# A state-space scan stage whose tensor-engine order is written out by hand, with 32-column output tiles

## The chip, the cores and the metric

One core of a Trainium2 chip (trn2) runs the whole program. The metric is the device time of one execution in microseconds (us), from start to end, as the median of several runs. PE is the tensor engine, DVE the vector engine, ACT the scalar engine, POOL the GpSimd engine, SP the engine that issues most DMAs. A PE matmul takes a stationary operand (loaded beforehand, up to 128x128) and streams a moving one through it into a PSUM bank; other engines must read PSUM before a bank can be used again.

## The reference

One decoder layer for a prompt of 512 tokens and 8 sample sequences of 8 tokens (576 tokens together, D = 1024): half a SwiGLU feed-forward, one wide input projection, a Mamba-2 state-space branch and an attention branch in parallel, their gated merge, an output projection, and half a SwiGLU again. The change concerns the state-space branch, cut here to what matters:

```
z, xbc, dt_raw, q, k, v, f_raw, g_ssd, g_att = split_combined(xn @ p['w_in'])
xc, conv_new = causal_conv(xbc, conv_prev, p['conv_w'], p['conv_b'])       # 4 taps, then SiLU
xs, Bm, Cm = jnp.split(xc, [D_SSM, D_SSM + SSD_GROUPS * D_STATE], axis=-1)  # 2048 + 4*128 + 4*128 columns
...
cb = jnp.einsum('bclgn,bcsgn->bclsg', Cc, Bc)
y_diag = jnp.einsum('bclsgr,bcsgrp->bclgrp', cb[..., None] * decay, xdt)
states = jnp.einsum('bclgn,bclgr,bclgrp->bcgrpn', Bc, jnp.exp(acs[:, :, -1:] - acs), xdt)
...
y_off = jnp.einsum('bclgn,bcgrpn,bclgr->bclgrp', Cc, h_prev, jnp.exp(acs))
y = (y_diag + y_off) + d_skip * xh
...
yg = y * silu(z); yg = yg * rsqrt(mean(yg * yg) + eps)                      # norm over each group
merged = sigmoid(g_ssd) * (y_ssd @ w_ssd_proj) + sigmoid(g_att) * (y_att @ w_attn_proj)
```

There are 32 heads of 64 channels in 4 groups; a chunk is 128 tokens, so the prompt has 4 chunks and the 64 sample tokens make a fifth.

## The kernel before

Activations lie transposed, channels on partitions and the 576 tokens along the free axis. Every large projection is a sum of three fp32r matmuls for each block of 128 input channels (`mm3`, lines 204 to 210): both operands are split into a high and a low part (`split` on lines 167 to 175 for weights, ACT makes the high part `whi`, DVE or POOL in turn the low part `wlo`), and high x high, high x low and low x high are added up in PSUM. A projection tile of 128 output channels covers the tokens in two halves of 288, each in a PSUM bank of its own (`acc`, two buffers): 24 matmuls a half for an input of 1024 channels, 12 for one of 512. DVE takes each half out of PSUM under `soon()`, which raises an instruction's priority for the scheduler.

The stages in order: first feed-forward; time steps and decays; attention, in which PE follows an order written by hand (`manual_schedule`, line 980) with half-tile pieces of other projections between its steps; group 0's convolutions and the attention output projection; the state-space scan; merge and output projection; second feed-forward. Outside the attention stage a scheduler sets the order of every engine, by its own estimate of when operands are ready. Each engine then works through its instructions strictly in that order.

The scan stage (line 1340 on) runs four groups. For each:

- `group_in(g)` (1078) makes six tiles with `conv_tile` (1036): the projections of B, C and four of x. The projection goes to `xr`; a PE transpose of its last columns into the second half's own bank (1059), copied out by ACT (`tt`, 1061), gives the new convolution state; ACT, three DVE steps of `kf` (1072), a tanh on ACT and two DVE writes (1074, 1076) give the convolved tile.
- `group_scan(g)` (1139) handles the samples as chunk 4 first and then chunks 0 to 3. `chunk` (1196) makes C.B (1202) and masks it into `cbm` (DVE, 1204), loads the cumulated decays `ab` by DMA, makes `dk` from them (ACT 1214 and 1215, DVE 1216), turns x (1225) and B (1232) by PE transposes, scales x to `xdt` and `xde` (DVE), and then forms y in one PSUM bank: for each of 8 heads one matmul of 64 columns from the chunk itself (1241) and, from chunk 1 on, one from the carried state (1243). DVE adds the skip (1245), and `gate` (1150) multiplies by the gate and sums squares on POOL and ACT. `carry` (1251) makes the next state, `state` (1265) updates one pair of heads of the samples' own states: transposes of a loaded state `h` (1273), an output product (1277), an update product (1280), and a DMA back.
- `halves` splits y into `ygh` and `ygl`; the samples' part is added and gated at the end of the group.
- `group_out(g)` (1320) finds the row scale of the group's norm (`rowscale`, 253: two matmuls with ones on lines 257 and 259, then a chain of small DVE operations up to 265), and projects y: 8 tiles with two halves of 12 matmuls, taken out by DVE (1331, 1334) and added to `accs` (1336).

The outer loop says in which order the work is written:

```
for g in range(4):
    cur = nxt
    gated = group_scan(g, *cur)
    if g < 3:
        nxt = group_in(g + 1)
    for _ in range((3, 0, 0, 5)[g]):
        j = next(late)
        gate_tile(gs, j, 8 + j)
    group_out(g, *gated)
```

The eight tiles of the gate projection (`gate_tile`, 507) are spare work: three go with group 0 and five with group 3.

PSUM banks in this stage: two `acc`, two `mm` (C.B, transposes of x and B, carry), two `tr` (states, row scales) and two `pv` (y and sample outputs).

## Time and profile before

| | us |
|---|---|
| runs shown (3) | 1911.07, 1919.22, 1919.95 |
| median | 1919.22 |
| the profiled execution | 1914.71 |
| its span, first to last instruction | 1912.9 |
| mean granted PE clock | 0.988 |

The profile is of one execution. Busy time counts an instruction's whole duration; matmuls are pipelined, so a busy PE may still work below its peak, and the time from one matmul's start to the next is the better measure. An fp32 matmul leaves two records, an fp32r matmul or a transpose one. In a row of a group, "idle before" is the time that the engine stood still just ahead of these instructions, and behind it stands what ended it. In a timeline row the first number is the start, the second the duration, "xN" the number of records merged, and a bracket gives the wait before it. A granted clock of 1.00 is full speed.

### The profile page before, as it was taken

How to read it: one execution, taken by the hardware profiler on the slowest of the kernel's cores; microseconds unless marked ns; L12 is line 12 of the kernel's file. 1: busy time of each engine (PE TensorE's matmuls, PEld its weight loads, DVE VectorE, ACT ScalarE, POOL GpSimd, SP SyncE). 2: the span in 40 equal slices, each digit the busy share in tenths (PEclk: the TensorE clock that was granted, in tenths of full speed). 3: DMA queues.
4: the chain of work that ended last, by engine and by line, in shares of the span. 5: the costliest groups of instructions: out<-in, count | busy, mean ns of one | idle time of the engine just before them, and what ended most of it. 6: DMA issues, size and time to landing. Idle time of an engine off the chain costs nothing. (4 is left out here: it accounts for less than half of the span.)

```text
span 1912.9 us, 38609 instructions
## 1 busy us (share of the span) xinstructions
PE 1840.0 (96%) x15335; PEld 1731.7 (91%) x15335; DVE 1065.6 (56%) x2204; ACT 748.2 (39%) x1553; POOL 652.2 (34%) x719
## 2 busy tenths in 40 slices
PE   7999999999998999999998988989999999999999
PEld 7999999999896888888997877878889999999998
DVE  4554334445234777775729767888785544334432
ACT  4233223334222555554427455555434333223322
POOL 0433012322322344432227455675744233003310
PEclk9999999999998999999999999999999999999999
DMA  5432223234534787865465545464654332222322
GB/s 152 112 96 80 89 78 89 83 105 111 145 109 129 188 255 223 246 200 148 95 174 153 141 127 142 111 178 124 174 155 136 89 88 77 80 74 81 88 90 71
DMA packets 270841, 243.21 MB, mean 127 GB/s; under 512 B 53276, under 2 KB 243404, under 8 KB 270508
## 3 DMA queue, kind: packets, MB, share of 16 engines
q1 hardware_dynamic: 208208, 169.35, 32.4%
q10 hardware_dynamic: 53092, 36.79, 6.4%
q0 software_dynamic: 9360, 34.61, 5.6%
q8 instruction: 121, 1.98, 0.4%
q14 instruction: 60, 0.49, 0.1%
HBM read 204.97 MB, written 29.03 MB: 122 GB/s over the span
## 5 line engine op out<-in xcount | busy, mean ns | idle before, releaser
L173 ACT ACTIVATE whi<-stage 128x512 fp32r<-128x512 f32 (+2 forms) x474 | 294.6, 622 | 732.4 <-PE acc L209 640.6
L208 PE MATMUL acc<-xh,whi 128*128 128x288 f32 x1856 | 561.7, 303 | 17.8 <-DVE xr L1046 11.5
L209 PE MATMUL acc<-xl,whi 128*128 128x288 f32 x1856 | 552.6, 298 | 0.0
L210 PE MATMUL acc<-xh,wlo 128*128 128x288 f32 x1856 | 552.3, 298 | 0.0
L174 DVE TENSOR_TENSOR wlo<-stage,whi 128x512 fp32r<-128x512 f32 (+1 forms) x373 | 271.9, 729 | 263.9 <-ACT whi L173 243.8
L208 PEld LDWEIGHTS acc<-xh,whi 128*128 128x128 f32 x1856 | 351.0, 189 | 24.8 <-DVE xr L1046 11.5
L209 PEld LDWEIGHTS acc<-xl,whi 128*128 128x128 f32 x1856 | 351.3, 189 | 2.1 <-issue 1.5
L210 PEld LDWEIGHTS acc<-xh,wlo 128*128 128x128 f32 x1856 | 350.7, 189 | 2.0 <-issue 1.3
L338 POOL TENSOR_TENSOR u<-u,s 128x288 f32<-128x288 f32 x88 | 92.1, 1048 | 484.3 <-DVE u L337 427.7
L208 PE MATMUL pv<-xh,whi 128*128 128x288 f32 (+1 forms) x784 | 231.4, 296 | 2.4 <-ACT xh L220 2.2
L209 PE MATMUL pv<-xl,whi 128*128 128x288 f32 (+1 forms) x784 | 231.9, 296 | 0.6 <-DVE xl L218 0.6
L210 PE MATMUL pv<-xh,wlo 128*128 128x288 f32 (+1 forms) x784 | 231.6, 296 | 0.0
L174 POOL TENSOR_TENSOR wlo<-stage,whi 128x512 fp32r<-128x512 f32 (+1 forms) x101 | 138.2, 1368 | 269.6 <-ACT whi L173 255.6
L208 PEld LDWEIGHTS pv<-xh,whi 128*128 128x128 f32 (+1 forms) x784 | 147.3, 188 | 2.9 <-ACT xh L220 2.4
L209 PEld LDWEIGHTS pv<-xl,whi 128*128 128x128 f32 (+1 forms) x784 | 147.2, 188 | 1.2 <-DVE xl L218 0.8
L210 PEld LDWEIGHTS pv<-xh,wlo 128*128 128x128 f32 (+1 forms) x784 | 147.2, 188 | 0.2
L340 POOL TENSOR_TENSOR hl<-u,hh 128x288 fp32r<-128x288 f32 x88 | 77.5, 882 | 81.6 <-ACT hh L339 81.6
L208 PE MATMUL pv<-hh,whi 128*128 128x288 f32 x352 | 104.4, 296 | 0.0
L209 PE MATMUL pv<-hl,whi 128*128 128x288 f32 x352 | 104.3, 296 | 0.0
L208 PE MATMUL acc<-hh,whi 128*128 128x288 f32 x352 | 104.1, 296 | 0.0
L210 PE MATMUL acc<-hh,wlo 128*128 128x288 f32 x352 | 104.1, 296 | 0.0
L209 PE MATMUL acc<-hl,whi 128*128 128x288 f32 x352 | 104.1, 296 | 0.0
(335 smaller groups left out, 3470.0 us busy)
## 6 DMA issues: line engine op xcount, KB each, us to landing
stage<-in_w_in_dram SPq DMA_DIRECT2D x52, 512.0 KB
stage<-in_ffn_w_up_dram SPq DMA_DIRECT2D x44, 512.0 KB
stage<-in_ffn_w_gate_dram SPq DMA_DIRECT2D x43, 512.0 KB
stage<-in_ffn_w_down_dram SPq DMA_DIRECT2D x40, 512.0 KB
pb<-pastD SPq DMA_DIRECT2D x32, 256.0 KB
ab<-cumD SPq DMA_DIRECT2D x32, 256.0 KB
h<-in_state_ssm_dram SPq DMA_DIRECT2D x32, 256.0 KB
out_dram<-h ACTq DMA_DIRECT2D x32, 256.0 KB
```

The source lines that it names most:

```text
L173: act(hi, view, AF.Copy)
L174: e.tensor_tensor(lo, view, hi.bitcast(F32), ALU.subtract)
L208: mm(out, lhsT=hi, rhs=a, start=first and i == 0, stop=False)
L209: mm(out, lhsT=hi, rhs=b, start=False, stop=False)
L210: mm(out, lhsT=lo, rhs=a, start=False, stop=last and i == n - 1)
L338: G.tensor_tensor(u, u, sil[half], ALU.mult)
L340: G.tensor_tensor(hl[:, hs(half)], u, hh[:, hs(half)].bitcast(F32), ALU.subtract)
```

## The change

The arithmetic stays the same. What changes is the code's order and, in the scan stage, who sets PE's order:

- `conv_tile` becomes a generator that yields after every 12 matmuls, and what follows the projection (transpose, copy, convolution steps) is put into a function `rest` that is called after the first piece of the next tile.
- `stream` runs a list of projection tiles as one stream of pieces, with the next tile's weights split and those of the tile after that loaded ahead. All projections of the stage go through it: each group's six tiles (`GroupIn`), the output projections (`GroupOut`) and the gate tiles.
- `group_scan` becomes a class `Scan` whose steps are called one by one: `front` (C.B, transposes, decays), `y`, `carry`, `state_load`, `state_turn`, `state_add`, `state_out`, `samples`, `final`. `front` transposes x and B straight behind C.B, ahead of the decays.
- In `y` each head's 64 output columns are made by two matmuls of 32 columns, and the order is four of the chunk's own, then four of the carried state, on the four column positions 0, 32, 64, 96.
- The whole stage stands in `manual_schedule` for PE: what the code writes is PE's order. Between the steps stand 12 slots a group, each filled with an equal share of the group's pieces. Group g's output projection now runs beside the scan of group g + 1, and the gate tiles are spread: two in group 0, one each in groups 1 and 2, four in group 3. The last group's output projection follows after the scan.

```diff
+    def halves_of(a, w, half):
+        for k in (0, 4):
+            mm3(a, w[k:k + 4], xs[k:k + 4], half, first=k == 0, last=k == 4)
+            if k == 0:
+                yield
...
-    def conv_tile(ct, w, prev, out):
+    def conv_tile(ct, w, prev, out, later):
...
         a = acc()
-        mm3(a, w, xs, 0)
+        yield from halves_of(a, w, 0)
         with soon():
             V.tensor_tensor(xr[:, 3:3 + HT], a, rbc[:, hs(0)], ALU.mult)
+        yield
...
+        def rest():
...
+        later.append(rest)
+        yield
...
+    def stream(jobs):
+        later = []
+        jobs[0][0].load(jobs[0][1])
+        ahead = jobs[0][0].get(jobs[0][1])
+        if len(jobs) > 1:
+            jobs[1][0].load(jobs[1][1])
+        for n, (_, _, body) in enumerate(jobs):
+            w, due, later = ahead, later, []
+            for c, _ in enumerate(body(w, later)):
+                if c == 0:
+                    for f in due:
+                        f()
+                    if n + 1 < len(jobs):
+                        ahead = jobs[n + 1][0].get(jobs[n + 1][1])
+                    if n + 2 < len(jobs):
+                        jobs[n + 2][0].load(jobs[n + 2][1])
+                yield
+        for f in later:
+            f()
...
-                for r in range(8):
-                    ov = yb[(r % 2) * 64:(r % 2 + 1) * 64, (r // 2) * n:(r // 2 + 1) * n]
-                    mm(ov, lhsT=xdt[:n, r, :], rhs=dks[r // 4][:n, r % 4, :n], start=True, stop=not 0 < c < 4)
-                    if 0 < c < 4:
-                        mm(ov, lhsT=hst[:, r, :], rhs=abs_[r // 4][:, r % 4, :], start=False, stop=True)
+                for i in range(4):
+                    for own in ((True, False) if 0 < c < 4 else (True,)):
+                        for e in range(2):
+                            r = 2 * i + e
+                            for q in range(2):
+                                o = e * 64 + q * 32
+                                ov = yb[o:o + 32, i * n:(i + 1) * n]
+                                if own:
+                                    mm(ov, lhsT=xdt[:n, r, q * 32:(q + 1) * 32], rhs=dks[r // 4][:n, r % 4, :n], start=True, stop=not 0 < c < 4)
+                                else:
+                                    mm(ov, lhsT=hst[:, r, q * 32:(q + 1) * 32], rhs=abs_[r // 4][:, r % 4, :], start=False, stop=True)
...
+        work = [[ins[1].job(i) for i in range(6)] + [gate_job(0), gate_job(1)],
+                [ins[2].job(0), ins[2].job(1)] + [outs[0].job(j) for j in range(8)] + [ins[2].job(i) for i in range(2, 6)] + [gate_job(2)],
+                [ins[3].job(0), ins[3].job(1)] + [outs[1].job(j) for j in range(8)] + [ins[3].job(i) for i in range(2, 6)] + [gate_job(3)],
+                [gate_job(4), gate_job(5)] + [outs[2].job(j) for j in range(8)] + [gate_job(6), gate_job(7)]]
...
+        with tc.manual_schedule(engines={mybir.EngineType.PE}):
+            for g in range(4):
...
+                sc.front(4)
+                fill()
+                if g:
+                    outs[g - 1].scale()
+                sc.front(0)
+                sc.state_load(0, 0)
+                fill()
+                sc.y(4, None)
+                for c in range(5):
+                    before = sc.carry(c) if c < 4 else None
+                    if c:
+                        sc.state_turn(c - 1)
+                    else:
+                        sc.state_load(1, 0)
+                    fill()
+                    if c < 3:
+                        sc.front(c + 1)
+                    if c:
+                        sc.state_add(c - 1)
+                        if c < 4:
+                            sc.state_load(0, c)
+                            sc.state_load(1, c)
+                    fill()
+                    if c < 4:
+                        sc.y(c, before)
+                    if c:
+                        sc.state_out(c - 1)
+                    if c == 2:
+                        sc.halves(0)
+                sc.final()
+                sc.samples()
+        outs[3].scale()
+        for _ in filler:
+            pass
```

Three places show how PE's order moves. A row has the line, the operation, output<-inputs, and the output's shape; L208 to L210 are projections, and a number behind a name tells one buffer from another.

The first is `front`. Before, in group 0, C.B of a chunk (L1202) is followed by y of the chunk ahead (L1241), then come the transposes of x (L1225) and of B (L1232):

```order
L1254 MATMUL mm_12518<-xde_12492,bt_12496 128x512
L1202 MATMUL mm_12560<-cT_11363,bT_11279 128x128
L1241 MATMUL pv_12498<-dk_12469,xdt_12490 64x128 x4
L1059 MATMUL acc_13072<-ident_76,xr_13043 91x128
L1241 MATMUL pv_12498<-dk_12478,xdt_12490 64x128 x4
L1225 MATMUL mm_12586<-ident_76,xg_11447 128x128 x4
L1232 MATMUL mm_12595<-ident_76,bT_11279 128x128
L1273 MATMUL tr_12525<-ident_76,h_2291_12523 128x128 x4
```

In the changed kernel C.B (L1261), the transposes of x (L1267) and of B (L1274) stand next to each other, and the samples' update products (L1363) follow:

```order
L1069 MATMUL acc_12828<-ident_76,xr_12723 91x128
L1261 MATMUL mm_12894<-cT_11364,bT_11295 128x128
L1267 MATMUL mm_12898<-ident_76,xg_11444 128x128 x4
L1274 MATMUL mm_12907<-ident_76,bT_11295 128x128
L1363 MATMUL tr_12933<-bs_12419,xs_12417 128x512
L1363 MATMUL tr_12937<-bs_12431,xs_12429 128x512
```

All three of `front`'s outputs are `mm` banks, of which there are two: the transpose of B takes the one that C.B was written to.

The second is y of chunk 1 of group 0, with 64-column tiles whose own and carried parts alternate (L1241 and L1243):

```order
L1280 MATMUL tr_12555<-bs_12447,xs_12445 128x512
L1241 MATMUL pv_12599<-dk_12566,xdt_12591 64x128
L1243 MATMUL pv_12599<-ab_12564,hst_12520 64x128
L1241 MATMUL pv_12599<-dk_12566,xdt_12591 64x128
L1243 MATMUL pv_12599<-ab_12564,hst_12520 64x128
```

and in the changed kernel with 32-column tiles in fours (L1314 and L1316), with the samples' outputs (L1373), the carry (L1328) and the state transposes (L1352) behind them:

```order
L1314 MATMUL pv_12985<-dk_12702,xdt_12692 32x128 x4
L1316 MATMUL pv_12985<-ab_12700,hst_12639 32x128 x4
L1314 MATMUL pv_12985<-dk_12702,xdt_12692 32x128 x4
L1316 MATMUL pv_12985<-ab_12700,hst_12639 32x128 x4
L1314 MATMUL pv_12985<-dk_12713,xdt_12692 32x128 x4
L1316 MATMUL pv_12985<-ab_12711,hst_12639 32x128 x4
L1314 MATMUL pv_12985<-dk_12713,xdt_12692 32x128 x4
L1316 MATMUL pv_12985<-ab_12711,hst_12639 32x128 x4
L1373 MATMUL pv_13030<-hT_12817,cz_12359 32x128 x4
L1373 MATMUL pv_13030<-hT_12825,cz_12359 32x128 x4
L1328 MATMUL mm_13040<-xde_12905,bt_12909 128x512
L1352 MATMUL tr_13045<-ident_76,h_2370_12941 128x128 x4
```

Twice as many matmuls make y, and no projection stands among them any more.

The third is the end of the last group's scan. Before, the transposes of the samples' output (L1302) and the first matmul of the row scale (L257) stand inside gate tiles (`xh`, `xl`):

```order
L1302 MATMUL tr_17209<-ident_76,oo_16761 128x128
L210 MATMUL acc_17448<-xh_4423,wlo_17440 128x288
...
L257 MATMUL tr_17565<-ssq_16683,cst_75 128x512
L210 MATMUL acc_17448<-xh_4770,wlo_17444 128x288
...
L259 MATMUL mm_17567<-ssq_16683,cst_75 128x64
L208 MATMUL acc_17511<-xh_4596,whi_17502 128x288
```

In the changed kernel no gate tile is left there, and the last output projection (`ygh`, `ygl`) follows at once:

```order
L1373 MATMUL pv_17782<-hT_17684,cz_12359 32x128 x4
L1398 MATMUL tr_17792<-ident_76,hst_17493 128x128 x4
L1385 MATMUL tr_17804<-ident_76,oo_17240 128x128 x3
L208 MATMUL acc_17854<-ygh_17475,whi_17729 128x288
...
L1385 MATMUL tr_17804<-ident_76,oo_17240 128x128
L257 MATMUL tr_17830<-ssq_16632,cst_75 128x512
L208 MATMUL acc_17876<-ygh_17475,whi_17729 128x288
L259 MATMUL mm_17832<-ssq_16632,cst_75 128x64
L209 MATMUL acc_17876<-ygl_17476,whi_17729 128x288
```

One half of a tile (acc_17854) stands between the samples' output and the row scale.

344 lines of the change are left out of this document (199 added, 145 removed).

## The prediction

> **What bounds the kernel now.** I read the page first, then a table of stages, then the groups of TensorE (PE) by line, and last the timeline at single places.
>
> ```profile
> PE 1840.0 (96%) x15335; PEld 1731.7 (91%) x15335; DVE 1065.6 (56%) x2204; ACT 748.2 (39%) x1553; POOL 652.2 (34%) x719
> ```
>
> PE is busy 96% of the span, so only what PE waits for, runs at a low clock, or spends on badly packed matmuls can be won. The stage table (columns: busy us and instructions of PE, weight loads, DVE, ACT, POOL; then granted clock, DMA share, GB/s) says where that is. 620:875 is the attention stage, whose PE order is written by hand already; 900:1000 holds group 0's convolutions; 1000:1432 is the scan with its projections, whose PE order the scheduler makes.
>
> ```profile
> 620.00:875.00 255.00, 249.28 (x3257) 213.72 (x3251) 192.69 (x563) 137.04 (x339) 100.17 (x129) 1.00 0.76 218
> 900.00:1000.00 100.00, 94.62 (x691) 92.57 (x690) 54.36 (x90) 33.38 (x54) 28.41 (x41) 0.98 0.46 119
> 1000.00:1432.00 432.00, 393.58 (x3140) 349.96 (x3139) 345.78 (x640) 227.85 (x525) 260.46 (x260) 0.98 0.52 146
> 1062.00:1080.00 18.00, 14.38 (x96) 12.43 (x94) 11.46 (x22) 9.79 (x24) 8.44 (x14) 0.81 0.59 143
> 1120.00:1136.00 16.00, 10.97 (x92) 9.57 (x90) 11.77 (x10) 4.19 (x10) 6.97 (x7) 0.89 0.45 121
> 1262.00:1280.00 18.00, 13.93 (x112) 11.31 (x112) 14.98 (x23) 13.39 (x36) 10.05 (x12) 0.91 0.57 144
> ```
>
> The scan stage leaves PE idle for 432 - 393.6 = 38.4 us, 9%; the hand-ordered attention stage for 255 - 249.3 = 5.7 us, 2.2%, at a similar DVE load (76% against 80%). What ends the waits in the scan stage, by group (idle is the last column):
>
> ```profile
> L208 PE MATMUL acc<-xh,whi 128*128 128x288 f32 x403 | 123.8, 307 | 13.2 <-DVE xr L1046 10.3 <-ACT tt L1061 2.3 <-ACT wdec L1135 0.5
> L208 PE MATMUL acc<-ygh,whi 128*128 128x288 f32 x253 | 78.1, 309 | 4.6 <-DVE u L1334 4.5
> L1241 PE MATMUL pv<-dk,xdt 128*64 128x128 f32 (+1 forms) x320 | 33.1, 280 | 8.8 <-DVE dk L1216 7.5 <-DVE xdt L1228 1.2
> ```
>
> Four single waits make 14.8 us of it:
>
> ```profile
> 1068.86 0.61 PE L208 MATMUL acc<-xh,whi 128*128 128x288 f32 x1 [3.55 <-DVE xr L1046]
> ...
> 1129.46 0.49 PE L1241 MATMUL pv<-dk,xdt 128*64 128x128 f32 x2 [5.03 <-DVE dk L1216]
> ...
> 1188.30 0.40 PE L208 MATMUL acc<-xh,whi 128*128 128x288 f32 x1 [3.09 <-DVE xr L1046]
> ...
> 1270.90 0.40 PE L208 MATMUL acc<-xh,whi 128*128 128x288 f32 x1 [3.17 <-DVE xr L1046]
> ```
>
> Three of the four have a low granted clock beside them (the last three rows of the table): 18 x 0.19 + 16 x 0.11 + 18 x 0.09 = 6.8 us of full clock.
>
> **The change, part by part.** Numbers of instructions stay the same on DVE, ACT, POOL and SP; PE alone gets more, smaller matmuls. The sum is made against the profiled execution, 1914.7 us (span 1912.9).
>
> *Waits that go.* With projection pieces between every step and its use, the four waits above and most small ones should go: all 38.4 us are up for removal. What is late next:
>
> (a) In `front`, the transpose of B (L1274) takes the PSUM bank that `cbm` is still read from, and only L1261 and four transposes stand between; nothing can pass it, and the whole stream behind it waits. DVE has to read `cbm`, often after an eviction of a projection:
>
> ```profile
> L1204 DVE TENSOR_TENSOR cbm<-mm,cst x20: 174/282/293, 995.1 to 1362.3; 128x128 f32<-128x128 f32 x16, 64x64 f32<-64x64 f32 x4
> ...
> L1334 DVE TENSOR_TENSOR u<-acc,ssq 128x288 f32<-128x288 f32 x46 | 20.8, 451 | 14.7 <-PE acc L210 8.1 <-POOL accs L1336 5.2 <-PE mm L1225 1.0
> ...
> L1072 DVE SCALAR_TENSOR_TENSOR kf<-xr,P,kf x72: 796/842/2022, 909.9 to 1316.4; 128x600 f32<-128x600 f32 x72
> ```
>
> How long the four transposes give it (from the first to the transpose of B, 0.49 us):
>
> ```profile
> 1017.44 0.66 PE L1225 MATMUL mm<-ident,xg 128*128 128x128 f32 x4
> 1017.93 0.27 PE L1232 MATMUL mm<-ident,bT 128*128 128x128 f32 x1
> ```
>
> 0.45 + 0.28 = 0.73 of DVE against 0.49 leaves 0.24 us; I take 0.45, for the hand-overs between engines and what else DVE has in hand, 20 times: 9 us. Bounds: 0, if DVE is free, and 20 x 1.1 = 22 if a convolution step (0.842) stands ahead as well.
>
> (b) The last convolution tile of a group is now followed by one gate tile alone in groups 1 and 2, and the next group's first transposes read it. I let its three steps (3 x 0.842) come out uncovered, twice: 5 us, bounds 0 and 16 (DVE having all of the group's start to do at once).
>
> (c) The end. Five gate tiles now run while the last samples are gated and the last row scale is found; the changed kernel has spent them earlier.
>
> ```profile
> 1387.43 0.27 PE L1302 MATMUL tr<-ident,oo 128*128 128x128 f32 x1
> ...
> 1391.80 0.32 POOL L1159 TENSOR_TENSOR ssq<-sq 128x64 f32<-128x64 f32 x1
> ...
> 1395.28 0.33 PE L259 MATMUL mm<-ssq,cst 128*128 128x64 f32 x2
> ...
> 1399.21 0.78 DVE L265 STREAM_TRANSPOSE ssq<-rsy 128x576 f32<-128x576 f32 x1
> ```
>
> From the transpose's end to the end of the sum of squares 4.4 us, from the L259 matmul to the end of L265 4.7, then an eviction 0.45: some 9.6 us. Two pieces of 12 matmuls (each about 0.13 us, 1.6 us a piece) can run in it before both accumulators are full, 3.1 us. The cover gone costs 6.5 us; bounds 4 and 10.
>
> (d) The waits of the output projections for DVE, 4.6 us, I leave as they are: their work is the same and stands at the same end.
>
> Waits that come back: 9 + 5 + 6.5 + 4.6 = 25. Won: 38.4 - 25 = 13 us. By attention's rate (2.2% of 432 = 9.5) plus (c) it would be 22; with the upper bounds of (a) to (c), 22 + 16 + 10 + 4.6 = 53, it is a loss of 14.
>
> *The clock.* Of the 6.8 us some lies under the waits; I take 5, and give 2 back for the wait at the end, which is longer than those that lowered it (the rows lost 1.6 to 3.4 each): 3 us won, bounds 0 and 5.
>
> *The output tiles.* Rows of y in 64-column tiles, whole and split by a projection, and of the 32-column tiles of attention:
>
> ```profile
> 1051.89 0.45 PE L1241 MATMUL pv<-dk,xdt 128*64 128x128 f32 x4
> ...
> 1053.84 0.40 PE L208 MATMUL acc<-xh,whi 128*128 128x288 f32 x1
> ...
> 1343.72 0.45 PE L1241 MATMUL pv<-dk,xdt 128*64 128x128 f32 x4
> 1343.99 0.40 PE L1243 MATMUL pv<-ab,hst 128*64 128x128 f32 x4
> 1344.21 0.38 PE L1241 MATMUL pv<-dk,xdt 128*64 128x128 f32 x2
> 1344.42 0.38 PE L1243 MATMUL pv<-ab,hst 128*64 128x128 f32 x2
> ...
> 1346.52 0.43 PE L1277 MATMUL pv<-hT,cz 128*32 128x128 f32 x8
> 1346.87 0.45 PE L1241 MATMUL pv<-dk,xdt 128*64 128x128 f32 x4
> ...
> 1348.33 0.70 PE L1254 MATMUL mm<-xde,bt 128*128 128x512 f32 x1
> ```
>
> ```profile
> 627.09 1.06 PE L810 MATMUL pv<-PT,vt 128*32 128x128 f32 x32
> 628.08 0.50 PE L779 MATMUL mm<-Ks,qs 128*128 128x256 f32 x2
> ...
> 641.24 0.62 PE L810 MATMUL pv<-PT,vt 128*32 128x128 f32 x16
> 641.79 0.50 PE L779 MATMUL mm<-Ks,qs 128*128 128x512 f32 x1
> ```
>
> A later chunk's y is 32 records (two a matmul): 1.95 us whole, about 0.9 + 1.46 split. A 32-column record costs (0.99 - 0.55) / 16 = 27 ns, plus 0.11 a block; 64 of them 1.86 us. So the narrow tile by itself wins 0.1 us. What wins is that the block is never split: 8 of the 12 are now (counted in the timeline), so 4 x 0.1 + 8 x 0.5 = 4.4. Behind it stands `state_out` in the same tiles; its 0.35 us falls by the 0.11 of a block, 12 times: 1.3. And PE goes between projections and other work 133 times in place of 225; going back costs some 0.1 us (the first projection matmul after a block, 1053.84, has 0.40 where others have 0.30), so half of 92 x 0.1 = 4.6. Together 10 us; bounds 4 and 13.
>
> By the Trainium skill, "TensorEngine Tiling (Array Packing)", Theoretical Speedup, tiles of 64 give up to 2x and tiles of 32 up to 4x. Read as a rate for one head that would halve y's 1.95 us and make the sum about 1875; a head of 64 columns needs two such tiles, though, and the rows above show no gain for it.
>
> *Group 0's convolutions* (900:1000, 5.4 us idle at a clock of 0.98): the transpose of the last rows now comes a piece later, so the next tile no longer waits at once for its copy (`tt`). I take 2.5 us; bounds 0 and 6.
>
> Sum: 13 + 3 + 10 + 2.5 = 28.5 us: 1914.7 - 28.5 = **1886**. The median of the runs shown is 1919.2 (1911.1 to 1920.0), 4.5 above the profiled execution, so a median may come out that much higher.
>
> **The rivals.**
>
> 1. *DVE becomes the bound.* It is busy 345.8 of 432 us; in 404 that is 86%. For it: one and the same convolution step takes 0.796 to 2.022 us, so DVE is held up by something, and closer packing may do it more often. 5% more DVE time is 17 us; if PE waits out most, 1886 + 13 = 1899. Against: the groups alternate between heavy and light stretches. The Trainium skill, "SBUF — State Buffer", SBUF: two separate sides, says that a DVE operation with two SBUF inputs and a GpSimd one exclude each other for a whole instruction, which speaks against this change; the spread of L1072 agrees. Chance 0.17.
>
> 2. *Slower: the fixed order waits on DVE at every `front`.* The mechanism is (a): PE stands at L1274 until DVE comes to `cbm`. If two long DVE steps stand ahead each time, 2.2 us x 20 = 44 in place of 9, and waits of over 2 us lower the clock again: 1886 + 35 + 3 = 1924. It ends the whole gain from 1.9 us a time (9 + 28.5 = 37.5 over 20), and is slower by over 0.5% from 2.35. For it: DVE is 80% busy there; against: it waits 14.7 us for u's sources alone, so it often stands idle for PE. Chance 0.12.
>
> 3. *The waits only move.* Idle time stays at 38 us since DVE's answers set it, and clock and front win nothing: 1914.7 - 10 = 1905, the edge of no change. For it: the scheduler already filled where it could; against: attention's 2.2%. Chance 0.13.
>
> 4. *The narrow tiles do run at twice the rate*, 1886 - 12 x 0.9 = 1875. The page just named would have it so. Against: the L810 rows. Chance 0.02.
>
> **How the numbers follow.** Forecast 1886 at 0.56. Faster by over 0.5% (9.6 us, about what a measurement tells apart): forecast, first and fourth rival, 0.75. Within 0.5%: the third, 0.13. Slower: the second, 0.12. The forecast's own bounds are 1914.7 - (25 + 5 + 13 + 6) = 1866 and, with (a) and (b) at their ends, past 1900; to hold 8 in 10 the range takes in the first rival and most of the third, and a little below the lower bound: 1864 to 1911.
>
> **What would show it.** Right: the stage from the first `front` to the last `ygh` matmul is some 25 us shorter, PE idle in it 25 us, the waits of 3 to 5 us gone but one of 5 to 7 us at the first output projections of group 3, y blocks of 1.9 us, DVE at 85%. Wrong: PE idle over 35 us with L1274 ended by `cbm` (rival 2) or spread over DVE operations that grew longer (rival 1); y blocks near 1 us (rival 4); or idle under 12 us, then (a) to (c) are too dear.

## The result, and the profile after

The changed kernel takes 1942.1 us (median of 4 runs, 1941.2 to 1943.1) beside 1919.6 us for the kernel before on the same chip. The ratio is 1.0126, with a 95% interval of 1.0095 to 1.0157: slower, where faster by 1.5% was forecast, and outside the range. The profiled execution has a span of 1941.3 us, 28.4 more than the one of before. Of all runs in this document one, of `warm` below, took 6004 us at a granted clock of 0.31, and it is in no ratio.

All of it lies in the scan stage. At 1000 us the two profiles stand within 2.2 us of each other in the program (17 projection matmuls), and both need 475 us from the last `ygh` matmul to the last matmul. First the stretches at half clock before, then the stage table (columns as in the prediction) for the changed kernel:

```profile
1067.40:1074.20 6.80, 5.34 (x27) 4.66 (x28) 3.81 (x6) 2.21 (x6) 1.06 (x4) 0.50 0.47 100
1128.80:1132.20 3.40, 2.74 (x25) 2.77 (x26) 2.44 (x5) 0.00 (x0) 0.00 (x0) 0.50 0.54 148
1272.20:1275.60 3.40, 3.40 (x17) 1.77 (x15) 3.36 (x6) 0.99 (x2) 1.81 (x1) 0.50 0.72 189
```

```profile
900.00:1000.00 100.00, 93.93 (x684) 91.55 (x682) 54.65 (x92) 33.51 (x54) 28.44 (x41) 0.98 0.47 121
...
1000.00:1461.80 461.80, 399.45 (x3679) 364.65 (x3679) 328.51 (x643) 227.01 (x525) 251.31 (x260) 0.95 0.50 138
1003.50:1013.70 10.20, 7.55 (x30) 6.91 (x31) 5.95 (x12) 5.85 (x18) 1.97 (x2) 0.50 0.54 147
1078.60:1082.00 3.40, 3.40 (x16) 3.40 (x15) 3.15 (x6) 3.05 (x9) 2.86 (x4) 0.50 0.94 243
1102.50:1109.30 6.80, 6.01 (x26) 6.01 (x27) 4.90 (x14) 2.00 (x4) 1.30 (x2) 0.50 0.33 85
1184.40:1187.80 3.40, 3.40 (x16) 3.38 (x15) 1.77 (x3) 0.63 (x1) 0.00 (x0) 0.50 0.81 225
1273.10:1276.50 3.40, 3.40 (x17) 3.40 (x16) 0.46 (x2) 2.63 (x7) 3.40 (x5) 0.50 0.00 0
1300.40:1303.80 3.40, 3.40 (x16) 3.40 (x15) 2.38 (x3) 0.63 (x1) 0.00 (x0) 0.50 0.94 265
1382.30:1385.80 3.50, 3.50 (x51) 3.07 (x53) 0.46 (x1) 0.00 (x0) 2.03 (x3) 0.51 0.41 117
1406.20:1409.70 3.50, 3.50 (x17) 3.50 (x16) 0.00 (x0) 0.70 (x2) 1.04 (x1) 0.51 0.00 0
1426.70:1437.00 10.30, 7.12 (x30) 6.77 (x30) 7.25 (x23) 1.45 (x3) 1.41 (x1) 0.50 0.15 32
```

The stage takes 461.8 us instead of 433.4 (1000 to the last `ygh` matmul). PE is idle for 461.8 - 399.45 = 62.3 us instead of 38.4. The nine lower rows are the stretches in which PE had half its clock: 47.8 us, against 13.7 before. PE was idle in 6.7 us of them, so they cost (47.8 - 6.7) / 2 = 20.5 us of work, against 5.8 before. The rest of the stage, work at full clock, is 378.9 us against 389.2, though 17 more projection matmuls fall into it (131 ns each, 2.2 us). So the change of 28.3 us is made up of:

| us | before | changed | difference | forecast |
|---|---|---|---|---|
| idle time of PE | 38.4 | 62.3 | +23.9 | -13 |
| lost to half clock | 5.8 | 20.5 | +14.7 | -3 |
| work at full clock | 389.2 | 378.9 | -10.3 | -10 |

What PE waits for, in the groups of PE by line over the stage (idle and its releasers are the last columns):

```profile
L208 PE MATMUL acc<-xh,whi 128*128 128x288 f32 x408 | 130.4, 319 | 10.5 <-DVE xr L1053 5.7 <-DVE u L1426 2.1 <-ACT tt L1071 1.6
L208 PE MATMUL acc<-ygh,whi 128*128 128x288 f32 x256 | 79.8, 312 | 17.5 <-DVE u L1426 13.3 <-ACT ygh L1226 2.3 <-DVE accs L1422 1.6
L1352 PE MATMUL tr<-ident,h 128*128 128x128 f32 x128 | 17.7, 278 | 7.3 <-DMA h<-in_state_ssm_dram 7.3
L1267 PE MATMUL mm<-ident,xg 128*128 128x128 f32 (+1 forms) x76 | 13.1, 299 | 6.9 <-DVE ssq L261 5.8 <-DVE hT L1272 1.2
L1261 PE MATMUL mm<-cT,bT 128*128 128x128 f32 (+1 forms) x38 | 7.9, 293 | 3.4 <-DVE cbm L1238 3.4
L1274 PE MATMUL mm<-ident,bT 128*128 128x128 f32 (+1 forms) x19 | 6.3, 330 | 10.9 <-DVE cbm L1263 9.2 <-DVE xde L1272 1.5
```

The waits for `dk`, 7.5 us before, are gone. In their place stand waits of many kinds: the accumulators (`u`, `xr`), the bank of `cbm`, the row scale's bank (`ssq`), the loads of the sample states. (At L1261 `cbm` is another tile in a buffer of that name, the low part of B that L1238 makes from the bank of the transposed B.) Twelve are over 2 us long, where before there were four.

How one of them comes about is seen in DVE's timeline, ahead of the PE wait of 3.15 us that ends at 1381.29 with `u` (start, duration, engine, line, operation; in brackets the idle time before it):

```profile
1372.60 0.28 DVE L1263 TENSOR_TENSOR cbm<-mm,cst 128x128 f32<-128x128 f32 x1
1375.49 0.81 DVE L1291 TENSOR_TENSOR dk<-dk,cbm 128x512 f32<-128x512 f32 x1 [2.61 <-ACT dk L1290]
1376.22 0.68 DVE L1270 TENSOR_TENSOR xdt<-mm,TT 128x512 f32<-128x512 f32 x1
1376.82 0.68 DVE L1272 TENSOR_TENSOR xde<-mm,wdec 128x512 f32<-128x512 f32 x1
1377.42 0.67 DVE L1364 TENSOR_TENSOR h<-h,tr 128x512 f32<-128x512 f32 x1
1378.02 1.18 DVE L1291 TENSOR_TENSOR dk<-dk,cbm 128x512 f32<-128x512 f32 x1
1379.12 0.67 DVE L1364 TENSOR_TENSOR h<-h,tr 128x512 f32<-128x512 f32 x1
1379.72 1.15 DVE L174 TENSOR_TENSOR wlo<-stage,whi 128x512 fp32r<-128x512 f32 x1
1380.79 0.81 DVE L1426 TENSOR_TENSOR u<-acc,ssq 128x288 f32<-128x288 f32 x2
```

And in the list of waits of the stage, two of DVE's own (us in total, times, longest):

```profile
DVE wlo L174 <- ACT whi L173: 23.4, 16, 8.7
DVE dk L1291 <- ACT dk L1290: 15.6, 8, 4.2
```

DVE itself stands at `dk` for 2.6 us, for ACT. Then seven steps that had gathered behind it run first, 5.3 us, and only then the eviction on which PE stands. PE had `y`, state steps and more in its queue, but behind the matmul that waited.

### The profile page after: what moved, and what is told of

Read it like the earlier page. It is cut to its first block, busy times and chain, and to the rows that moved or that the text cites. A ratio compares the mean times of both kernels' runs of the same rounds, so it can differ in the third digit from the quotient of the medians.

```text
span 1941.3 us, 39604 instructions
## 1 busy us (share of the span) xinstructions
PE 1841.7 (95%) x15847; PEld 1741.5 (90%) x15847; DVE 1044.0 (54%) x2204; ACT 747.8 (39%) x1553; POOL 644.1 (33%) x719
## 5 line engine op out<-in xcount | busy, mean ns | idle before, releaser
L208 PE MATMUL acc<-xh,whi 128*128 128x288 f32 x1856 | 566.9, 305 | 15.1 <-DVE xr L1053 6.9
L210 PE MATMUL acc<-xh,wlo 128*128 128x288 f32 x1856 | 554.4, 299 | 0.0
L174 DVE TENSOR_TENSOR wlo<-stage,whi 128x512 fp32r<-128x512 f32 (+1 forms) x373 | 262.2, 703 | 269.0 <-ACT whi L173 251.1
L208 PEld LDWEIGHTS acc<-xh,whi 128*128 128x128 f32 x1856 | 355.4, 192 | 20.6 <-ACT tt L1071 6.6
L209 PEld LDWEIGHTS acc<-xl,whi 128*128 128x128 f32 x1856 | 355.5, 192 | 1.9 <-issue 1.0
L210 PEld LDWEIGHTS acc<-xh,wlo 128*128 128x128 f32 x1856 | 354.8, 191 | 0.5
L208 PE MATMUL pv<-xh,whi 128*128 128x288 f32 (+1 forms) x784 | 231.2, 295 | 0.7 <-ACT xh L220 0.5
L210 PE MATMUL pv<-xh,wlo 128*128 128x288 f32 (+1 forms) x784 | 231.3, 295 | 0.0
L208 PEld LDWEIGHTS pv<-xh,whi 128*128 128x128 f32 (+1 forms) x784 | 147.1, 188 | 1.3 <-ACT xh L220 0.8
L210 PEld LDWEIGHTS pv<-xh,wlo 128*128 128x128 f32 (+1 forms) x784 | 146.9, 187 | 0.2
L208 PE MATMUL pv<-hh,whi 128*128 128x288 f32 x352 | 104.4, 297 | 0.0
L210 PE MATMUL acc<-hh,wlo 128*128 128x288 f32 x352 | 104.1, 296 | 0.0
L208 PE MATMUL acc<-hh,whi 128*128 128x288 f32 x352 | 104.1, 296 | 0.0
```

The source lines that it names most:

```text
L174: e.tensor_tensor(lo, view, hi.bitcast(F32), ALU.subtract)
L208: mm(out, lhsT=hi, rhs=a, start=first and i == 0, stop=False)
L209: mm(out, lhsT=hi, rhs=b, start=False, stop=False)
L210: mm(out, lhsT=lo, rhs=a, start=False, stop=last and i == n - 1)
```

## The experiments

Each kernel was run beside the kernel before on one chip; the ratio is to that. The stage is counted from 1000 us to the last `ygh` matmul, its parts worked out as above. In the column of work, 131 ns is taken off for each projection matmul that the window holds beyond the kernel before's. Switches are those of PE between projections and other work. The times in the expectations count from 1942 us for the changed kernel beside 1919.6 before; to hold a run against them, its ratio is multiplied by 1919.6, since the kernel before took 1912.7 to 1919.6 us from chip to chip.

| kernel | ratio to before, 95% | stage | idle | half clock | lost by it | work | switches |
|---|---|---|---|---|---|---|---|
| before | 1 | 433.4 | 38.4 | 13.7 | 5.8 | 389.2 | 214 |
| changed | 1.0126 [1.0095, 1.0157] | 461.8 | 62.3 | 47.8 | 20.5 | 376.5 | 121 |
| sched | 1.0026 [1.0013, 1.0039] | 441.2 | 30.9 | 30.7 | 11.3 | 394.9 | 210 |
| narrow_before | 0.9969 [0.9953, 0.9984] | 431.5 | 28.3 | 20.5 | 9.7 | 389.3 | 218 |
| wide_after | 1.0106 [1.0078, 1.0134] | 457.6 | 53.6 | 51.2 | 22.3 | 377.9 | 122 |
| one_bank | 1.0116 [1.0087, 1.0145] | 453.5 | 59.6 | 41.0 | 17.0 | 374.5 | 121 |
| light_after | 1.0076 [1.0047, 1.0106] | 447.8 | 48.8 | 51.2 | 21.5 | 375.3 | 121 |
| light_before | 0.9913 [0.9885, 0.9942] | 413.8 | 21.6 | 3.4 | 1.7 | 389.6 | 216 |
| early_y | 1.0221 [1.0190, 1.0251] | 468.3 | 68.2 | 47.8 | 19.2 | 378.5 | 121 |
| edges | 1.0102 [1.0074, 1.0131] | 453.6 | 56.4 | 41.0 | 17.9 | 377.1 | 125 |
| fine | 1.0127 [1.0102, 1.0151] | 455.9 | 54.0 | 44.0 | 20.4 | 379.2 | 257 |
| mended | 1.0151 [1.0128, 1.0175] | 464.5 | 62.0 | 58.0 | 24.9 | 376.9 | 124 |
| warm | 1.0090 [1.0056, 1.0124] | 449.6 | 50.6 | 30.7 | 14.4 | 382.3 | 121 |
| scan_first | 1.0181 [1.0160, 1.0202] | 469.0 | 67.8 | 58.0 | 20.9 | 374.8 | 123 |
| rest_late | 1.0114 [1.0094, 1.0134] | 459.9 | 61.6 | 47.8 | 18.8 | 376.1 | 122 |
| first_bank | 1.0135 [1.0115, 1.0155] | 467.8 | 62.5 | 61.4 | 26.2 | 375.3 | 126 |
| nb_bank | 0.9990 [0.9979, 1.0000] | 430.0 | 32.7 | 17.1 | 7.6 | 389.1 | 220 |
| nb_dk | 0.9966 [0.9949, 0.9984] | 429.2 | 27.8 | 13.7 | 5.2 | 393.6 | 214 |
| nb_dk2 | 0.9969 [0.9956, 0.9982] | 433.3 | 26.1 | 17.1 | 7.4 | 392.4 | 214 |
| nb_whole | 0.9935 [0.9916, 0.9954] | 428.4 | 30.7 | 17.1 | 7.8 | 384.3 | 190 |

### Which part of the change: the order, or the code and tiles

The theory was that the written order itself does it (A); the rivals were the new code (B) and the many small matmuls (C).

```diff
-        with tc.manual_schedule(engines={mybir.EngineType.PE}):
+        if True:
```

> The changed kernel, but TensorE's order in the scan stage is again made by the scheduler; pieces, job list, output tiles and all other code as in the changed kernel. Theory A (the written order makes TensorE stand in line at steps whose answer is not there yet, and each wait of 2 to 4 us lowers the clock after it): idle time of TensorE in the stage falls from 62 to about 40 us, half-clock time from 48 to under 20 us, 1900 to 1915 us. Rival B (the pieces, the postponed convolution steps and the earlier gate tiles do the harm, whoever orders them): 1935 to 1945 us, idle about 60. Rival C (twice as many small matmuls lower the clock): half-clock time stays near 48 us, 1925 to 1935 us.

The other two swap the block of y matmuls between the kernels. For `narrow_before`, with n, c, xdt and the rest as they are in the kernel before:

```diff
-                for r in range(8):
-                    ov = yb[(r % 2) * 64:(r % 2 + 1) * 64, (r // 2) * n:(r // 2 + 1) * n]
...
+                for i in range(4):
+                    for own in ((True, False) if 0 < c < 4 else (True,)):
+                        for e in range(2):
+                            r = 2 * i + e
+                            for q in range(2):
+                                o = e * 64 + q * 32
...
```

> The changed kernel with y in 64-column tiles as before, in the written order. Theory A: a block of a later chunk goes from 1.77 to about 1.95 us, 12 times, so 1942 to 1947 us, idle and half-clock time as in the changed kernel. Rival C (the many small matmuls lower the clock): half-clock time falls to under 25 us, 1925 to 1932 us.

> The kernel before with y in 32-column tiles, nothing else. Theory A: whole blocks fall from 1.95 to about 1.8 us, split ones hardly, and the order may shift a little: 1908 to 1922 us, half-clock time in the stage under 20 us. Rival C: half-clock time over 30 us, 1925 to 1935 us.

The stage row of `sched`, and the groups that held the most of the idle time in the changed kernel:

```profile
1000.00:1441.20 441.20, 410.32 (x3695) 360.85 (x3695) 334.27 (x643) 226.56 (x525) 255.52 (x261) 0.97 0.51 145
```

```profile
L208 PE MATMUL acc<-xh,whi 128*128 128x288 f32 x413 | 126.4, 306 | 3.1 <-DVE xr L1053 2.7 <-ACT wdec L1186 0.4
L208 PE MATMUL acc<-ygh,whi 128*128 128x288 f32 x256 | 83.2, 325 | 13.4 <-DVE u L1426 10.8 <-ACT ygh L1226 2.3
L1314 PE MATMUL pv<-dk,xdt 128*32 128x128 f32 (+1 forms) x640 | 39.4, 273 | 7.3 <-DVE dk L1291 5.4 <-DVE xdt L1270 1.9
```

With the changed kernel's code and the scheduler's order back, idle time is 30.9 us, half of the changed kernel's and less than before's; the waits for `cbm` are gone but for 0.5 us, and those for `dk` are back (5.4). B falls as the main cause, but not wholly: the ratio is 1.0026, so of the 1.26% some 0.3% is the new code's and 1.0% the written order's. The 1925 us this makes are above A's range, since the half-clock time fell to 30.7 us and not under 20, and work is dearer (394.9 us against 389.2). The one line also changes more than PE's order: the scheduler makes the other engines' orders around it, and those of DVE, ACT and GpSimd come out different too. No run holds them fixed. C falls: under the scheduler narrow tiles gave 0.3%, with 20.5 us of half clock, and 64-column tiles in the written order left it at 51.2 us. The 64-column tiles did not cost the few us expected either (the intervals overlap).

### One wait at a time

> The changed kernel, but the transpose of B is written into a free part of the bank that holds C.B, right behind it, so nothing on TensorE waits there for the read of C.B. Theory A (waits everywhere, this is one of six kinds): the 10.9 us at that transpose go, with some half-clock time; a part comes back at the x transposes and the next evictions: 1925 to 1937 us. Rival D (this bank is the main harm and sets off the others): 1900 to 1912 us. Rival E (waits only move): idle stays near 62 us, 1938 to 1945 us.

```diff
                 mm(s[:n, :n], lhsT=bT[:, o0:o0 + n], rhs=cT[:, o0:o0 + n], start=True, stop=True)
+                nc.tensor.transpose(s[:n, P:2 * P], bT[:, o0:o0 + n], ident)
...
-                t = sm()
-                nc.tensor.transpose(t[:n, :P], bT[:, o0:o0 + n], ident)
```

> The changed kernel with two starts mended: in group 0 the first pieces of the stream run ahead of the first front, and the row scale's 64-column product goes to a bank of the y kind, so that no x transpose waits for its read. Theory A (each wait has its own cause, and can be taken away by itself): 6.1 us of idle at 1003 to 1008 and 5.8 us at the row scales go, with 10 to 17 us of half clock: 1922 to 1931 us. Rival E (waits only move, as in the run with one bank): idle stays above 58 us, 1935 to 1943 us.

```diff
-            t2 = sm()
+            t2 = side()                      # pv for the group's row scale, sm elsewhere
...
+                if g == 0:
+                    fill()                   # 13 places in group 0
                 sc.front(4)
```

> The changed kernel with each chunk's y ahead of the next chunk's front, not behind it, so that the three tiles of ab and of dk come free a half step earlier (two tiles belong to a chunk, so the second of the next chunk can only be loaded behind y). Theory H (operands one step ahead with buffers for one and a half make VectorE stand at dk, and u behind it): SyncE's wait for pv at the ab load falls from 16 us to under 6, the u waits fall by 5 to 8 us, 1925 to 1935 us. Rival (the front, and with it cbm and the transposes, comes half a step later in relation to its use and nothing is gained): 1937 to 1947 us.

```diff
                     fill()
+                    if c < 4:
+                        sc.y(c, before)
                     if c < 3:
                         sc.front(c + 1)
...
-                    if c < 4:
-                        sc.y(c, before)
```

The waits of PE in `one_bank`, then in `early_y` (what was waited for; us in total, times, longest; the last row is DVE's):

```profile
PE acc L208 <- DVE u L1425: 18.5, 12, 3.8
PE tr L1351 <- DMA h<-in_state_ssm_dram: 12.7, 3, 6.1
```

```profile
PE mm L1274 <- DVE cbm L1263: 15.6, 14, 3.2
PE tr L1352 <- DMA h<-in_state_ssm_dram: 12.3, 4, 6.4
PE acc L208 <- DVE u L1426: 9.9, 7, 3.8
PE tr L1352 <- DVE kf L1082: 9.8, 2, 5.6
...
DVE dk L1291 <- ACT dk L1290: 2.7, 3, 1.5
```

In `one_bank` the wait at the transpose of B is gone, but idle time is 59.6 us: `u` went from 15.5 to 18.5, the state loads from 7.3 to 12.7. Rival E is what happened (1942 us); D falls, and with it the thought that this bank is the harm. In `edges` the waits at the row scale are gone, and at the start those of 3.4 us at line 1261 and 1.2 at line 1267, but the one for `cbm` at line 1274 went from 9.2 to 18.0 us, 3.0 of them at the start; idle time is 56.4 us, and the ratio is not clear of the changed kernel's. In `early_y` DVE's wait for `dk` fell from 15.6 to 2.7 us and that for `u` by 5.6, as H has it, but SyncE's wait for pv at the `ab` load rose from 15.9 to 32.2 us, `cbm`, the state loads and `kf` took the place, and it has the highest ratio of all. Where a wait is mended, the time comes back at another.

> The changed kernel with three mends together: B transposed into the bank of C.B, y ahead of the next front, and the two starts of the run named edges. Theory A (each wait has its own cause; y early freed ab but put 19 us on cbm, which the one bank takes away): idle falls to 35 to 45 us, 1912 to 1925 us. Rival E (the waits move on to the state loads and accumulators): idle stays above 52 us, 1930 to 1945 us.

`mended` holds the edits of `one_bank`, `early_y` and `edges` together: idle 62.0 us, ratio 1.0151. The state loads alone hold 16.4 us in it. The remedies do not add up.

### Is it DVE's load, its order, or the grain

> The changed kernel with two of the three multiply-add steps of each convolution tile left out (36 of VectorE's operations in the scan stage, some 33 us of its time; the output is not the reference's). Theory F (TensorE's waits for u, xr, cbm, ssq and accs, 46 of its 62 us, are a backlog of VectorE, that stands ahead of the eviction TensorE waits for): idle falls by 20 us or more, with the clock the time falls to 1900 to 1915 us. Rival G (VectorE itself stands at steps whose input is late, and would with less work too): idle falls by under 8 us, 1930 to 1940 us.

> The same steps left out of the kernel before, to tell what the lighter VectorE is worth where the scheduler orders TensorE. Theory F: less than in the changed kernel, since the scheduler has put other matmuls over the backlog: idle falls from 38 to about 28 us, 1900 to 1910 us. Rival G: 1912 to 1920 us, as little as in the changed kernel.

```diff
-            for j in range(1, 4):
+            for j in range(1, 2):
                 V.scalar_tensor_tensor(cv[:, :m], xr[:, j:j + m], wc(j), cv[:, :m], ALU.mult, ALU.add)
```

The stage row of `light_after`, then that of `light_before`:

```profile
1000.00:1447.80 447.80, 399.05 (x3677) 365.40 (x3678) 293.65 (x606) 227.05 (x525) 244.96 (x260) 0.94 0.50 141
```

```profile
1000.00:1413.80 413.80, 392.22 (x3157) 349.38 (x3156) 298.47 (x606) 227.35 (x525) 250.62 (x260) 1.00 0.54 154
```

With 35 us less on DVE in 448, it is busy 66% of the stage, and PE still idles for 48.8 us at no better clock. That is 13.5 us less idle time, more than G allowed (8) and less than F asked for (20); the 1934 us are G's, and the gain of 0.5% is not clear of noise, as the intervals overlap. Under the scheduler's order the same edit gives 0.9%, more and not less, and takes idle time to 21.6 us. So DVE's load has a part in the backlog but is not the main matter: F falls.

> The changed kernel with the same steps in a finer written order: front in two parts, and a piece or two of the stream between any two steps (31 places a group in place of 12). Theory K (the clumps do it: front, state_add, y and state_out stand back to back, so VectorE gets 4 to 8 us of work at once, the steps that read their results and the two accumulators wait for it, and a lighter VectorE does not help since the clump stays): idle falls from 62 to 35 to 45 us, half-clock time to under 30 us, and some 100 more switches cost about 10 us of work: 1918 to 1930 us. Rival L (a written order of whatever grain waits, since it does not know when the other engines answer): idle stays above 55 us, 1940 to 1955 us.

```diff
+                fill()
+                sc.back(c + 1)               # front from the transpose of B on
...
-        SLOTS = 12
+        SLOTS = 31
```

Idle time is 54.0 us (a further 4.1 us of wait, at line 1261, ends just ahead of 1000 us), and the ratio is 1.0127 as in the changed kernel: 1944 us, which is L's. `cbm` gave way to `xr` (14.9 us at line 1069). The number of switches, 257, is even above the scheduler's, and work is only 2.7 us more than in the changed kernel, where some 10 were expected. The grain alone does not make the difference; K falls.

> The changed kernel, TensorE's order unchanged, with high priority for the scan's own steps (front, y, carry and the state steps) on the other engines, the priority that the evictions have already. Theory P (the scan's steps on VectorE stand behind convolution steps and splits of the stream, since their places in the program are mixed, and TensorE waits in line for them): the waits for cbm fall from 12.8 to under 5 us, for u and xr by some, idle to 40 to 48 us, 1915 to 1930 us. Rival Q (VectorE's order is not the cause; a written order does not fit the times at which the engines answer): idle stays at 55 to 65 us, 1934 to 1945 us.

```diff
+                with soon():
                     sc.front(4)              # and y, carry, state_turn, state_add, state_out
```

> The changed kernel with lowered priority for the postponed convolution steps of the stream, the other side of the same question. Theory P: as the run scan_first, idle 40 to 50 us, 1915 to 1932 us. Rival Q: 1934 to 1945 us; or slower, 1945 to 1955 us, where the convolution steps come late for the next front.

```diff
                     for f in due:
-                        f()
+                        with tc.high_priority(offset=off):      # -3000 in the scan stage
+                            f()
```

> The changed kernel with the scan's steps at high priority, B in the bank of C.B, and the two mended starts (one_bank, edges). Theory P: the three add up, since what each takes away is no longer refilled: idle 28 to 38 us, 1900 to 1915 us. Rival Q: idle above 50 us, 1930 to 1945 us.

Idle 67.8, 61.6 and 62.5 us, and `scan_first` (1.0181) is slower than the changed kernel: neither of the two priorities tried on the other engines' side mends it, alone or with the bank and the starts (`first_bank` holds the edits of `scan_first`, `one_bank` and `edges`). P falls.

### Does a wait cost the clock after it

> The changed kernel with matmuls of no use (their results are not read) put into three kinds of wait: 22 of 288 columns, some 2.9 us, ahead of the first chunk's front in groups 0 and 1 (waits of 3.4 and 4.0 us), and 14 at the end of the written order, ahead of the last output projections (wait of 2.3 us). Theory M (it is the wait that lowers the clock after it, so a wait also costs half of what follows): the half-clock time at 1003, 1102 and 1427 us falls by 15 to 20 us, the time by 5 to 10 us, though TensorE does more: 1930 to 1937 us. Rival N (the clock falls for another reason, the mix of matmuls or what the chip draws): half-clock time stays near 48 us and the time goes up by 0 to 5 us, 1941 to 1947 us.

```diff
+        def warm(n):
+            t = pv()
+            for _ in range(n):
+                mm(t[:, :HT], lhsT=xs[0][0][:, :P], rhs=xs[0][1][:, :HT], start=True, stop=True)
...
+                if g < 2:
+                    warm(22)                 # behind the first fill of the group
...
+            warm(14)                         # behind the last samples
```

In the stage table of `warm`, the start, the place of the 4 us wait, and the half-clock stretch at the end:

```profile
1000.00:1449.60 449.60, 398.98 (x3718) 364.53 (x3717) 326.98 (x637) 226.73 (x523) 252.61 (x260) 0.97 0.49 140
1002.00:1012.00 10.00, 7.45 (x66) 7.10 (x70) 6.42 (x12) 6.06 (x17) 2.39 (x3) 0.83 0.52 135
1098.00:1112.00 14.00, 13.51 (x122) 12.05 (x120) 12.51 (x36) 6.99 (x18) 3.57 (x5) 1.00 0.49 134
1417.90:1424.70 6.80, 5.53 (x23) 5.53 (x24) 4.62 (x9) 0.68 (x1) 1.40 (x1) 0.50 0.16 40
```

At the three places half clock fell from 10.2, 6.8 and 10.2 us to 3.4, 0 and 6.8: 17 us, as M has it, with 58 matmuls more. The smaller idle time (50.6 us) is in part these matmuls, which count as work. The profiled execution is 12 us shorter; the ratio, 1.0090, has an interval that overlaps the changed kernel's, so a gain in time is not certain.

### What can be kept

> The kernel before with 32-column tiles of y and with B transposed into the bank of C.B (one bank fewer to wait for in each chunk): what of the change may be kept without the written order. Theory A (waits at this bank come from the written order alone): as the kernel before with narrow tiles, 0.995 to 0.999 of before, 1904 to 1914 us. Rival (fewer banks in use let the scheduler run ahead): idle falls under 24 us, 1895 to 1903 us.

> The kernel before with 32-column tiles of y and the second of the two decay products of a chunk (dk by cbm, 16 times) on GpSimd in place of VectorE, which takes some 14 us from VectorE and adds 20 to 30 to GpSimd (260 us busy of 433). If a lighter VectorE is what the scheduler's order turns into time (light_before: 33 us less gave 17), 0.990 to 0.995 of before, 1893 to 1903 us; if GpSimd answers later than VectorE did, or holds VectorE up, 0.998 to 1.006, 1908 to 1924 us.

> The run nb_dk (32-column tiles of y, the second decay product on GpSimd, the scheduler's order) with high priority for the gate of the samples, on whose sum of squares TensorE waited 8.3 us there. If the wait goes: 5 to 8 us less, 0.992 to 0.994 of before, 1898 to 1905 us. If GpSimd is late anyway, or the wait moves: 0.995 to 0.999.

> The kernel before with 32-column tiles of y and high priority for the y matmuls, so that the scheduler does not split a block by projections. If the unbroken blocks are worth what the changed kernel's work shows and the waits stay the scheduler's: 2 to 5 us under the run narrow_before (0.9969 of before), 0.994 to 0.996. If y then stands in line for its decay products: idle rises from 28 to 35 or more, 0.998 to 1.006.

```diff
+                with soon():
                     for i in range(4):
                         for own in ((True, False) if 0 < c < 4 else (True,)):
```

`nb_whole` is `narrow_before` with that line around the y matmuls, `nb_bank` with the bank of `one_bank`, and the two others with the edit below; `nb_dk2` also puts `soon()` around the gate of the samples.

```diff
-                    V.tensor_tensor(dv, dv, cbm[:n, :n]
+                    (G if r0 and c < 4 else V).tensor_tensor(dv, dv, cbm[:n, :n]
```

The bank and GpSimd's share bring nothing beyond the narrow tiles, and in `nb_dk2` the wait for the samples' sum of squares stayed (8.3 us, then 7.4). `nb_whole` is faster than both kernels, 0.9935 of before: in its profile projections stand inside one of the 12 blocks of chunks 1 to 3 and not four, work is 5 us less than in `narrow_before` (384.3 against 389.3), idle time 2.4 more. That it is also faster than `narrow_before` is likely, but the two intervals touch.

## Why the prediction was wrong, point by point

**The step that failed** is the first under "Waits that go": "With projection pieces between every step and its use, the four waits above and most small ones should go: all 38.4 us are up for removal." Its support was the attention stage's 2.2%. The sum left 25 us of idle time; 62.3 were measured. Of the four waits only the one for `dk` went for good; `xr` still has 9.0 us (5.7 and 3.3), and other waits came that the sum held at nothing. With a fixed order, a step whose answer is late holds up everything behind it. The start of the stage shows this: DVE stands for the same load (`acsD`) in both kernels, 4.82 us to 1000.72 before and 4.58 us to 1001.78 in the changed kernel, but PE was idle 0.47 us for it before, and 3.40 us at L1261 in the written order. Every order written here, coarse or fine, left 49 to 68 us idle; every kernel with the scheduler's order has 22 to 38. That it is the order written for PE, with what the scheduler makes of the others' around it, and neither the tiles nor in the main the code, is shown by `sched`.

**(a) The transpose of B behind `cbm`**: 9 us forecast, 9.2 measured. The mechanism was right, but that the size came out is partly luck: it was put at 0.45 us for each of 20, and was four waits of 1.4 to 2.3 us and four under 0.6, with none at the other twelve. What the second rival made of it was wrong: without this wait the time is not clearly different (`one_bank`). It is a sign of the lateness, not its source.

**(b) The last convolution tile**: 5 us forecast. No `front` of groups 2 and 3 waited for a convolution step; what PE met at the group starts was the row scale's bank (L1267, 5.8 us, 4.0 of them in group 1), which the sum did not have: the row scale's second matmul (L259) writes to one of the two `mm` banks, not to a `tr` bank.

**(c) The end**: 6.5 us forecast; the waits from 1420 on are

```profile
1424.60 0.40 PE L208 MATMUL acc<-ygh,whi 128*128 128x288 f32 x1 [2.33 <-ACT ygh L1226]
...
1430.94 0.61 PE L208 MATMUL acc<-ygh,whi 128*128 128x288 f32 x1 [3.19 <-DVE u L1426]
```

0.40 at the row scale's L259 and two of about 1 us behind them, 8 us in all. Right, within its bounds of 4 and 10.

**(d) The evictions of the output projections**, left at 4.6 us: `u` and `accs` have 15.5 and 2.7, some 5 of them counted under (c). The DVE timeline above is one of them.

**Left out**: the loads of the sample states, 7.3 us. In the written order their transposes stand at a fixed place, while the load stands in SyncE's queue behind weight loads that wait for buffers (0.96 and 3.02 us for `wlo` in the case below), and then waits for its own, 1.64 us more:

```profile
1395.12 3.85 SPq L161 DMA_DIRECT2D stage<-in_w_ssd_proj_dram  x2
1400.66 0.37 SPq L1344 DMA_DIRECT2D h<-in_state_ssm_dram  x1
```

PE came to its transposes at 1401.4 and waited 4.59 us, to 1406.03.

**The clock**: 3 us to be won were forecast, 14.7 were lost. The sum took the clock as something that goes with the waits that go, and put 3 us on it in the second rival; in fact ten of the twelve waits over 2 us have 3.4 us or more of half clock at or behind them, and there are eight such waits more than before. The sum had put no price on the clock behind a wait that comes anew.

**The output tiles and switches**: 10 us forecast, 10.3 measured, 12.7 with the projections counted alike. The sum was right; its parts were not, so that is partly luck. A block of a later chunk takes 1.77 us (1283.69 to 1285.46), not 1.86, and none of the 12 is split. Of the 8 blocks split before, 5 have projections inside and 3 only other small work. The 4.6 us for switches are not borne out: `fine`, with 136 switches more than the changed kernel, has 2.7 us more work. `wide_after` has 377.9 us of work, so the tiles are some 1.4 us of the 12.7; how the rest divides between unbroken blocks and the order of the other small work is not shown.

```profile
1283.69 0.43 PE L1314 MATMUL pv<-dk,xdt 128*32 128x128 f32 x8
...
1285.46 0.62 PE L1373 MATMUL pv<-hT,cz 128*32 128x128 f32 x16
```

**Group 0's convolutions**: 2.5 us forecast, none came; 900:1000 has 6.1 us idle where it had 5.4.

**The rivals.** The first (DVE becomes the bound, its operations longer) did not happen: DVE is busy 328.5 us of the stage, less than before (345.8), and the convolution step did not grow, 1.00 us in the mean of the stage (1.09 before, on L1072):

```profile
L1082 DVE SCALAR_TENSOR_TENSOR kf<-xr,P,kf 128x600 f32<-128x600 f32 x54 | 54.0, 1000 | 6.2 <-ACT kf L1080 4.2 <-POOL wlo L174 1.4
```

The second had the sign and the kind, waiting in line for DVE and the clock with it, but put it at one place and stopped at 1924 us. The third said that waits only move; they moved and grew. The fourth is ruled out by the block's 1.77 us. None had waits at six kinds of places at once. The forecast's own upper bound on what is won, 25 us of waits, is given without a working; its own lower bounds on (a) to (d) (0, 0, 4 and 4.6) would make it 38.4 - 8.6 = 29.8.

**What stays open.** Why so many answers come late for a written order, though DVE has less to do, is not settled. Load, two priorities, one bank, the grain and the starts have been tried one by one. DVE's own waits are not the answer by themselves: in the changed kernel it stands for `dk` 15.6 us and for `whi` 23.4, but under the scheduler's order, in `sched`, 17.8 and 20.8, and in `early_y`, with the highest ratio, `dk` has only 2.7. What is left is the fit of the orders of the engines to each other: under the scheduler PE has something else to do in such a wait, under a written order it stands behind it. That is argued from the timelines, not shown. A written order that copies the scheduler's places, the other engines' orders held fixed, and more buffers for `ab`, `dk` and the states were not tried.

## What to carry to other kernels

A wait that a scheduler leaves can be the smaller of two evils: before an order is written by hand for a stage where five engines answer each other, ask of each place in it what comes if that one answer is 2 us late, and price it with the clock behind it. Test the order apart from the code that comes with it; here one line told them apart. And look whether the part that pays, here narrow tiles in unbroken blocks, can be had by a priority alone.

## What the runs showed of the hardware

PE's clock fell after shorter waits than those of the profile before (3.1 to 5.0 us). Of the seven waits of 2.1 to 2.5 us in the changed kernel, five are followed within 2.2 us by a half-clock stretch and two are not. One of each:

```profile
1052.46 0.33 PE L1274 MATMUL mm<-ident,bT 128*128 128x128 f32 x1 [2.17 <-DVE cbm L1263]
```

```profile
1078.15 0.71 PE L1352 MATMUL tr<-ident,h 128*128 128x128 f32 x4 [2.12 <-DMA h<-in_state_ssm_dram]
```

By the Trainium skill, "TensorE: Matmul & The Clock Gate", HAM oscillation, idle gaps of more than about 3.4 us are what lowers the clock; here waits of 2.1 to 2.5 us did so five times in seven, so the trace does not agree with that bound.

What tells the two apart is where the wait lies. The starts of the nine stretches in the stage table are all a whole number of steps of 3.413 us apart (1003.5 and 1078.6, for example, by 22), as if the clock were set anew at each step. These rows are one step each, the last step ahead of the drop at 1078.6 and the step that holds the end of the wait at 1052.46:

```profile
1075.14:1078.56 3.42, 1.30 (x21) 0.90 (x13) 3.38 (x6) 0.00 (x0) 1.15 (x1) 1.00 0.56 122
1051.25:1054.67 3.42, 2.21 (x15) 2.12 (x16) 3.42 (x7) 3.26 (x9) 2.96 (x5) 1.00 0.01 2
```

In the first PE was busy 38% of the step, and the clock fell; the second wait is cut by a step's edge, PE was busy 72% and 65% of the two steps, and it did not. Over the twenty profiles, the 141 half-clock stretches from 950 to 1470 us all begin on such steps, each profile's counted from its own first, and in all but one of them PE was busy at most 56% of the step ahead (64% in the other); no step at full clock under 44% was followed by one at full clock. So what counted here was about half a step's work, not the length of a single wait. That filling waits with matmuls of no use keeps the clock up is what `warm` shows, 27.2 us of half clock at three places against 10.2.
